# SSD products of four heads in one visit, retention's products by kind, an extra step between retention's scores and their use, and later last blocks of the norms

## The chip, the cores and the metric

The kernel runs on one core of one Trainium2 chip. TensorE (PE) does the matrix products, VectorE (DVE), ScalarE (ACT) and GpSimd (POOL) the rest, and SyncE (SP) issues the transfers. The metric is the device time of one execution in microseconds (us), the median of several runs.

## The reference

A hybrid encoder of two layers is applied to a prompt of 512 tokens and a sample of 256 tokens, with a width of 1024, in fp32. The even layer mixes with an SSD scan of 16 heads (two groups of 8, both directions) and with retention of 8 heads (both directions), the odd layer with dilated attention and a gMLP. Each layer then has a squared-ReLU MLP. Every mixer and MLP stands between an RMS norm before and one after. Cut to what matters here:

```python
def ssd_chunked(x, log_a, bm, cm):                      # chunks of 128 tokens
    ...
    cb = jnp.einsum('bclgn,bcsgn->bcgls', cc, bc)
    y_diag = jnp.einsum('bcgels,bcsgep->bclgep', cb[:, :, :, None] * decay, xc)
    ...
    y_off = jnp.einsum('bclgn,bcgepn,bcgel->bclgep', cc, h_in, jnp.exp(a_cs).astype(x.dtype))
    return (y_diag + y_off).reshape(Bsz, L, G, E, P)

def retention_chunked(q, k, v, log_gamma):
    ...
    scores = jnp.einsum('bclhd,bcshd->bchls', qc, kc) * dmat
    y_in = jnp.einsum('bchls,bcshv->bclhv', scores, vc)
    ...
    y_cross = jnp.einsum('bclhd,bchdv,hl->bclhv', qc, r_in, q_decay)
    return (y_in + y_cross).reshape(Bsz, L, H, DV)

def even_mixer(h, in_proj, ...):
    ...
    y = y_f + y_b + xs * d_skip.reshape(SSD_GROUPS, SSD_HPG, 1).astype(xs.dtype)
    y_ssd = gated_group_rms(y.reshape(Bsz, S, SSD_WIDTH), z, ssd_norm_w)
    ...
    y_ret = head_group_norm(r, ret_gn_w) * jax.nn.silu(g)
    return jnp.concatenate([y_ssd, y_ret], axis=-1) @ out_proj

def trunk(x, norm_mix_pre, norm_mix_post, ...):
    for i in range(DEPTH):
        h = rms_norm(x, norm_mix_pre[i])
        ...
        x = x + rms_norm(mix, norm_mix_post[i])
        h = rms_norm(x, norm_ffn_pre[i])
        f = jnp.square(jax.nn.relu(h @ ffn_w1[i])) @ ffn_w2[i]
        x = x + rms_norm(f, norm_ffn_post[i])
    return x
```

## The kernel before

**Precision.** A big projection multiplies operands split in two parts (whi and wlo of a weight, h or mh in a high and a low part), so that one product is three matmuls (L156 to L158, L191 to L193, L212 to L214). L118 loads a weight, ACT makes its high part (L121) and DVE the low one (L122). SSD and retention products are plain fp32, each issued as a pair.

**What sets the order.** PE's order is written out by hand: it is the order of the code. `weave(steps, fill, per)` walks through the steps of a special stage (SSD or retention) and puts `per` steps of a projection's matmuls, the fill, behind each `yield`. A fill step is 6 matmuls. When the fill is used up, the steps stand alone. The other engines' orders come from a scheduler that follows the code and takes `high_priority()` work first. All transfers go through SP's one queue, in order. PSUM has three pools: dps with 3 tiles for projections, mps with 3, tps with 2. A tile is held until its last reader is done.

**SSD** (`ssd`, once per head group g). Chunks of 128 tokens, six in all. Before the products of chunk c, the code makes the products C B' (cb, L1297) and the masks of chunk c + 1: `ssd_decay` loads decays (rr), masks and exponentiates them, POOL adds the two directions (L1360), DVE multiplies by cb (L1361, the mask product) and adds the D-skip on the diagonal (four steps of L1365). The products L1315 then run in four visits per chunk, two heads each: terms ea with hf (state from the left), ea with hb (from the right), rr with xtok (inside the chunk), 64 output rows a head, so the tile is 128*64. The norm of a chunk has two halves (L1374 sums the squares; L1382 spreads the result); they stand between the products of the next chunk and ahead of those of the one after.

**Retention** (`ret`, once per head group of four). First the states (rl with rs, L1507, and on DVE L1516 and L1522), then for each of six chunks `ret_chunk`: transposes L1537 and L1543, scores L1552 (64 rows), the masked scores sct on DVE (L1557), half of the norm of the chunk before, products L1565 (sct with v) and L1566 (qst with the states ri; 64 rows in the first and the last chunk of a sequence, 128 otherwise, since ri stacks the two directions). `ret_norm` normalises ys (L1579 to L1588), transposes (L1591) and stores the mix tile. Fill of retention group 0 are the projections of group 1 (`E.gates(1)`, `E.ret_proj`), 3.6 steps each, and fill of group 1 is three quarters of the output projection (`out(0)` to `out(2)`, which load mix tiles, mh, L1612 to L1618), 2.4 each. The last quarter follows group 1, with tiles of its own.

**Norms behind a projection** (`PostNorm`). Of each of three token blocks the squares are summed (ACT L456, POOL L460, PE L276), then `end` makes r (L285 to L290), scales (L486), adds the residual (L490) and makes the next projection's h (L364, L365). For the last block, `pre.rest()` calls it from within the next projection, behind its first dense unit of 24 matmuls (`units_a` L145, `units_b` L179). In the last norm of the program nothing follows: eight scales L486 and eight adds L490 end the kernel.

```python
                if i == j == 0 and not pre.first:
                    pre.rest()
```

## Time and profile before

| what | value |
|---|---|
| three runs, median | 2264.56 us (2263.85 to 2268.53) |
| profiled execution, its own time | 2263.86 us |
| its span, first to last instruction | 2262.1 us |
| mean granted clock of PE | 0.990 |
| PE busy (matmuls) | 2191.4 us, 97% |
| PE weight loads | 2027.0 us, 90% |
| DVE busy | 1679.8 us, 74% |
| ACT busy | 1056.9 us, 47% |
| POOL busy | 614.4 us, 27% |

A matmul's duration in a row of the trace is longer than the distance to the next one, since matmuls overlap in the array; the stream is read from the starts. PE's stream has no slack of its own, so what counts are the places where the distance between two starts is larger than it should be.

### The profile page before, as it was taken

Reading aid. Unit: us, or ns where it says so; the run is one execution under the profiler, and the core shown is the slowest. Engines: PE = TensorE matmul, PEld = TensorE weight load, DVE = VectorE, ACT = ScalarE, POOL = GpSimd, SP = SyncE. Lnnn points to the kernel's source line nnn. Section 1 sums busy time; section 2 is a strip of 40 time slices with the busy share of each in tenths; the row PEclk is TensorE's granted clock in tenths of the full one; section 3 lists DMA queues with packets and bytes.
Section 4 is the critical chain, followed back from the end, with each engine's and each line's share of the span. In section 5 each row is a group of like instructions: output and inputs, shape, how many; then the busy total and the mean of one; then the engine's idle time right before and its main releaser. Section 6 shows DMA issues by size and latency. Waiting matters only on the chain.

```text
span 2262.1 us, 39158 instructions
## 1 busy us (share of the span) xinstructions
PE 2191.4 (97%) x14360; PEld 2027.0 (90%) x14360; DVE 1679.8 (74%) x3538; ACT 1056.9 (47%) x2132; POOL 614.4 (27%) x617
## 2 busy tenths in 40 slices
PE   8998999999999999999999999999999999999997
PEld 7877888998889999989988988888988999999987
DVE  8969858646658776687677858788767776687676
ACT  6646455334335544454244415555655544454242
POOL 2335234311104144311404030011004154311404
PEclk9999999999999999999999999999999999999999
DMA  4435235446434343454353345444634343454342
GB/s 150 120 125 170 88 102 167 149 136 192 136 107 142 97 142 123 143 184 145 114 170 119 109 140 171 147 157 133 193 112 132 104 137 123 143 189 140 114 152 89
DMA packets 188897, 311.23 MB, mean 138 GB/s; under 512 B 18913, under 2 KB 119329, under 8 KB 188705
## 3 DMA queue, kind: packets, MB, share of 16 engines
q1 hardware_dynamic: 188704, 308.73, 43.1%
q8 instruction: 113, 1.85, 0.3%
q14 instruction: 80, 0.65, 0.1%
HBM read 234.64 MB, written 74.02 MB: 136 GB/s over the span
## 4 chain that ended last, share of the span: by engine, by line
PE 62%; DVE 18%; DMA 9%; issue 4%; ACT 4%; POOL 2%; SPq 1%; POOLq 0%; ACTq 0%; DVEq 0%
PE dps L156 4%; PE dps L157 4%; PE dps L158 4%; PE dps L212 4%; PE dps L213 4%; PE dps L214 4%; PE dps L191 3%; PE dps L192 3%; PE dps L193 3%; PE dps L663 3%; PE dps L664 3%; PE dps L665 3%; DMA raw<-in_f 2%; DVE wlo L122 2%; PE mps L665 2%
## 5 line engine op out<-in xcount | busy, mean ns | idle before, releaser
L212 PE MATMUL dps<-mh,whi 128*128 128x256 f32 (+1 forms) x800 | 271.6, 340 | 1.4 <-DVE acc L223 1.1
L213 PE MATMUL dps<-mh,whi 128*128 128x256 f32 (+1 forms) x800 | 266.1, 333 | 0.0
L214 PE MATMUL dps<-mh,wlo 128*128 128x256 f32 (+1 forms) x800 | 265.3, 332 | 0.0
L191 PE MATMUL dps<-whi,h 128*128 128x256 f32 x864 | 260.8, 302 | 0.2 <-ACT rv L1466 0.2
L156 PE MATMUL dps<-h,whi 128*128 128x256 f32 (+1 forms) x728 | 251.8, 346 | 0.0
L192 PE MATMUL dps<-wlo,h 128*128 128x256 f32 x864 | 246.3, 285 | 0.0
L193 PE MATMUL dps<-whi,h 128*128 128x256 f32 x864 | 246.3, 285 | 0.0
L158 PE MATMUL dps<-h,wlo 128*128 128x256 f32 (+1 forms) x728 | 242.8, 333 | 0.0
L157 PE MATMUL dps<-h,whi 128*128 128x256 f32 (+1 forms) x728 | 242.1, 333 | 0.0
L122 DVE TENSOR_TENSOR wlo<-raw,whi 128x1024 fp32r<-128x1024 f32 x140 | 177.1, 1267 | 45.1 <-ACT whi L121 44.5
L121 ACT ACTIVATE whi<-raw 128x1024 fp32r<-128x1024 f32 x140 | 147.6, 1056 | 123.4 <-PE dps L157 49.6
L191 PEld LDWEIGHTS dps<-whi,h 128*128 128x128 f32 x864 | 166.6, 193 | 11.3 <-issue 8.5
L192 PEld LDWEIGHTS dps<-wlo,h 128*128 128x128 f32 x864 | 166.9, 193 | 3.3 <-issue 2.2
L212 PEld LDWEIGHTS dps<-mh,whi 128*128 128x128 f32 x800 | 152.7, 191 | 18.8 <-DVE acc L223 2.7
L193 PEld LDWEIGHTS dps<-whi,h 128*128 128x128 f32 x864 | 166.8, 193 | 0.0
L214 PEld LDWEIGHTS dps<-mh,wlo 128*128 128x128 f32 x800 | 152.4, 191 | 14.8
L213 PEld LDWEIGHTS dps<-mh,whi 128*128 128x128 f32 x800 | 152.9, 191 | 13.3
L460 POOL TENSOR_TENSOR sq<-sq 128x256 f32<-128x256 f32 x79 | 64.9, 822 | 342.9 <-ACT sq L456 342.3
L156 PEld LDWEIGHTS dps<-h,whi 128*128 128x128 f32 x728 | 138.1, 190 | 17.0 <-issue 4.9
L157 PEld LDWEIGHTS dps<-h,whi 128*128 128x128 f32 x728 | 138.3, 190 | 13.6 <-issue 1.7
L158 PEld LDWEIGHTS dps<-h,wlo 128*128 128x128 f32 x728 | 137.9, 189 | 13.6
L223 DVE TENSOR_TENSOR acc<-acc,dps 128x512 f32<-128x512 f32 (+1 forms) x208 | 100.5, 486 | 66.0 <-PE dps L214 65.7
(380 smaller groups left out, 6323.7 us busy)
## 6 DMA issues: line engine op xcount, KB each, us to landing
raw<-in_f SPq DMA_DIRECT2D x128, 512.0 KB, 3.8
hidD<-hc SPq DMA_DIRECT2D x104, 192.0 KB, 1.9
xt<-hidD SPq DMA_DIRECT2D x40, 384.0 KB, 3.6
rr<-acsD SPq DMA_DIRECT2D x48, 256.0 KB, 3.6
raw<-in_evB SPq DMA_DIRECT2D x24, 512.0 KB, 3.7
rl<-retD SPq DMA_DIRECT2D x48, 256.0 KB, 2.8
raw<-hidD SPq DMA_DIRECT2D x24, 512.0 KB, 3.9
stk<-qkD SPq DMA_DIRECT2D x96, 128.0 KB, 2.8
```

The costliest lines, as they stand in the source:

```text
L121: nc.scalar.activation(out=hi, in_=raw, func=AF.Copy)
L122: nc.vector.tensor_tensor(out=lo, in0=raw, in1=hi, op=ALU.subtract)
L156: nc.tensor.matmul(o, lhsT=hi[:, k, :], rhs=hh[k][:, sl], start=k == 0, stop=False)
L157: nc.tensor.matmul(o, lhsT=hi[:, k, :], rhs=hl[k][:, sl], start=False, stop=False)
L158: nc.tensor.matmul(o, lhsT=lo[:, k, :], rhs=hh[k][:, sl], start=False, stop=k == NKT - 1)
L191: nc.tensor.matmul(o, lhsT=hh[k][:, sl], rhs=hi[:, k % 4, :], start=k == 0, stop=False)
L192: nc.tensor.matmul(o, lhsT=hh[k][:, sl], rhs=lo[:, k % 4, :], start=False, stop=False)
L193: nc.tensor.matmul(o, lhsT=hl[k][:, sl], rhs=hi[:, k % 4, :], start=False, stop=k == NKT - 1)
L212: nc.tensor.matmul(o, lhsT=hi[:, k, ms], rhs=hh[k][:, sl], start=k == 0, stop=False)
L213: nc.tensor.matmul(o, lhsT=hi[:, k, ms], rhs=hl[k][:, sl], start=False, stop=False)
L214: nc.tensor.matmul(o, lhsT=lo[:, k, ms], rhs=hh[k][:, sl], start=False, stop=k == 3)
L665: nc.tensor.matmul(o, lhsT=lo[:, k, :], rhs=hh[k], start=False, stop=last and k == 3, **f)
```

## The change

It has five parts.

1. `units_a` and `units_b` call `pre.rest()` one dense unit later: behind the second one and not the first. It concerns the MLP of both layers and the odd layer's input projection.
2. In the last block of the last norm, r is written to a PSUM tile (tps) instead of SBUF.
3. SSD: the two `yield` of two heads move behind those of four heads, so a chunk has two visits instead of four. The second half of a norm (`yield from spread`) moves from before the products to behind them. cb moves from tps to mps. The D-skip becomes one wide add per four heads, of a table (`di`) that 8 steps per group make ahead. The mask product gets high priority.
4. More tiles for s0 (6 instead of 4), and the last quarter's mh tiles lie in tiles that are dead by then.
5. Retention: a step (`yield`) now stands between scores and their use. All four qst products run first, then all four sct products. The half norm of the chunk before moves from between scores and use to behind the products and a step. The masked scores get high priority. Each chunk so has one more step, and takes one more helping of fill.

```diff
@@ units_a, units_b
-                if i == j == 0 and not pre.first:
+                if i == 0 and j == 1 and not pre.first:
                     pre.rest()
...
-                    if c == 0 and w is ws[0]:
+                    if c == 1 and w is ws[0]:
                         pre.rest()
@@ PostNorm.end
-        r = T.rstd(st, n, eps=None if self.eps is None else self.eps[s][:, c0 // CH:(c0 + n) // CH])
+        y = T.tps()[:, 0:n] if self.prek is None and b == BLOCKS[-1] else None
+        r = T.rstd(st, n, y, eps=None if self.eps is None else self.eps[s][:, c0 // CH:(c0 + n) // CH])
@@ Even.diagonals, called ahead of back_states(0) and, for group 1, behind the weave of ssd(0)
+    def diagonals(self, g):
+
+        self.di = []
+        for q in range(2):
+            t = self.pool.tile([128, 512], F32, tag="di", name="di", bufs=2)
+            for i in range(4):
+                h = 64 + 8 * g + 4 * q + i
+                self.nc.vector.tensor_scalar(out=t[:, 128 * i:128 * i + 128], in0=self.T.ident,
+                                             scalar1=self.rows[:, h:h + 1], scalar2=None, op0=ALU.mult)
+            self.di.append(t)
@@ ssd
-                cb = T.tps()
+                cb = T.mps()
...
-            yield from spread
             if c < 0:
                 continue
...
-                    yield
+
+                yield
+                yield
                 if q == 0:
                     yield from islice(half, 1)
+            yield from spread
             spread = half
@@ ssd_decay
-        nc.vector.tensor_tensor(out=v3(m), in0=v3(m), in1=cb[:, 0:128].unsqueeze(1).to_broadcast([128, 4, 128]),
-                                op=ALU.mult)
-        for i in range(4):
-            sl = slice(128 * i, 128 * i + 128)
-            nc.vector.scalar_tensor_tensor(out=m[:, sl], in0=T.ident, scalar=self.rows[:, 64 + h0 + i:65 + h0 + i],
-                                           in1=m[:, sl], op0=ALU.mult, op1=ALU.add)
+        with T.tc.high_priority():
+            nc.vector.tensor_tensor(out=v3(m), in0=v3(m), in1=cb[:, 0:128].unsqueeze(1).to_broadcast([128, 4, 128]),
+                                    op=ALU.mult)
+            nc.vector.tensor_tensor(out=m, in0=m, in1=self.di[q], op=ALU.add)
@@ ret_chunk
-        yield from half
+        yield
         y = T.mps()
         rows = slice(64 if c == c0 else 0, 64 if c == c1 else 128)
-        for h in range(4):
-            hs = slice(128 * h, 128 * h + 128)
-            nc.tensor.matmul(y[:, hs], lhsT=st[:, hs], rhs=v[:, hs], start=True, stop=False)
-            nc.tensor.matmul(y[:, hs], lhsT=qst[rows, hs], rhs=ri[rows, hs], start=False, stop=True)
+
+        for a, b, r, f in ((qst, ri, rows, True), (st, v, slice(0, 128), False)):
+            for h in range(4):
+                hs = slice(128 * h, 128 * h + 128)
+                nc.tensor.matmul(y[:, hs], lhsT=a[r, hs], rhs=b[r, hs], start=f and h == 0, stop=not f and h == 3,
+                                 skip_group_check=True)
...
         yield
+        yield from half
```

How the instructions move is seen at three places. In the changed kernel the lines are a little further down: L1315 is L1326, L1297 is L1308, L1382 is L1394, L1507 is L1519, L1565 and L1566 are L1580, L1586 and L1588 are L1601 and L1603, L1591 is L1606, L1618 is L1633.

PE, the products of one chunk's first four heads in SSD group 0, before (ea, hf, hb, rr and xtok as above; each row of L1315 is a pair of products, and issues two matmuls for each):

```order
L158 MATMUL dps<-h,wlo 128x512
L1315 MATMUL mps<-ea,hf 64x128 x2
L1315 MATMUL mps<-ea,hb 64x128 x2
L1315 MATMUL mps<-rr,xtok 64x128 x2
L156 MATMUL dps<-h,whi 128x512
...
L158 MATMUL dps<-h,wlo 128x512
L1315 MATMUL mps<-ea,hf 64x128 x2
L1315 MATMUL mps<-ea,hb 64x128 x2
L1315 MATMUL mps<-rr,xtok 64x128 x2
L156 MATMUL dps<-h,whi 128x512
```

The same after. The two visits have become one, and the six fill matmuls between them stand behind it:

```order
L158 MATMUL dps<-h,wlo 128x512
L1326 MATMUL mps<-ea,hf 64x128 x2
L1326 MATMUL mps<-ea,hb 64x128 x2
L1326 MATMUL mps<-rr,xtok 64x128 x2
L1326 MATMUL mps<-ea,hf 64x128 x2
L1326 MATMUL mps<-ea,hb 64x128 x2
L1326 MATMUL mps<-rr,xtok 64x128 x2
L156 MATMUL dps<-h,whi 128x512
```

PE, from the last products of retention group 0 (chunk 5) to the states of group 1, before. The row of L1591 is the norm's transposes of chunk 5 (sct is the tile that the normalised values are written to), rs the scaled keys; between the products and L1591 there are 72 fill matmuls of the projections, and the fill of group 1 (L212 on) begins with the states:

```order
L1565 MATMUL mps<-rl,sct 128x128
L1566 MATMUL mps<-ri,qst 128x128
L191 MATMUL dps<-whi,h 128x256
...
L1591 MATMUL tps<-ident,sct 128x128 x4
L191 MATMUL dps<-whi,h 128x256
...
L1507 MATMUL mps<-rl,rs 128x128 x4
L212 MATMUL dps<-mh,whi 128x512
...
L1507 MATMUL mps<-rl,rs 128x128 x4
```

The same after. Behind the products there is one step of fill (6 matmuls) and then the transposes of chunk 4; the states of group 1 follow, and only behind these, with 48 fill matmuls of L212 to L214 between and behind them, the transposes of chunk 5:

```order
L193 MATMUL dps<-whi,h 128x256
L1580 MATMUL mps<-ri,qst 128x128 x4
L1580 MATMUL mps<-rl,sct 128x128 x4
L191 MATMUL dps<-whi,h 128x256
...
L193 MATMUL dps<-whi,h 128x256
L1606 MATMUL tps<-ident,sct 128x128 x4
L1519 MATMUL mps<-rl,rs 128x128 x4
...
L1519 MATMUL mps<-rl,rs 128x128 x4
L212 MATMUL dps<-mh,whi 128x256
...
L1606 MATMUL tps<-ident,sct 128x128 x4
L212 MATMUL dps<-mh,whi 128x512
```

DVE, the last steps of the norm of chunk 5 (L1586, L1588) and what follows them, up to the first masked scores of group 1 (L1557), before. gx belongs to the gates, mh and wlo to the output projection, de to the decay tables of group 1:

```order
L1586 TENSOR_SCALAR sct<-ys,mv,rsq_y 128x128 x3
L1473 TENSOR_SCALAR gx<-dps,rc_101 128x256
L1586 TENSOR_SCALAR sct<-ys,mv,rsq_y 128x128
L1588 TENSOR_TENSOR sct<-sct,rl 128x512
...
L1618 TENSOR_TENSOR mh<-raw,mh 128x512
...
L1618 TENSOR_TENSOR mh<-raw,mh 128x256 x3
L122 TENSOR_TENSOR wlo<-raw,whi 128x1024
L1432 SCALAR_TENSOR_TENSOR de<-de,trif 128x128
...
L1618 TENSOR_TENSOR mh<-raw,mh 128x512 x3
...
L1557 TENSOR_TENSOR sct<-dm,mps 128x2x128 x2
```

The same place after: the norm's statistics, weights, decay tables and states of group 1 (ri) all stand ahead of the norm's last steps (L1601, L1603), for which the transposes of chunk 5 wait:

```order
L1633 TENSOR_TENSOR mh<-raw,mh 128x512
...
L1594 BN_STATS bs<-ys 128x6
...
L122 TENSOR_TENSOR wlo<-raw,whi 128x1024
...
L1444 SCALAR_TENSOR_TENSOR de<-de,trif 128x128
...
L1528 SCALAR_TENSOR_TENSOR ri<-ri,gam,mps 64x128 x5
L122 TENSOR_TENSOR wlo<-raw,whi 128x1024
L1528 SCALAR_TENSOR_TENSOR ri<-ri,gam,mps 64x128 x3
L265 SCALAR_TENSOR_TENSOR rsq_y<-rsq_u,rsq_y 128x4
L1601 TENSOR_SCALAR sct<-ys,mv,rsq_y 128x128 x4
L1534 SCALAR_TENSOR_TENSOR ri<-ri,gam 64x128
L1603 TENSOR_TENSOR sct<-sct,rl 128x512
```

## Rows read from the trace of the kernel before

**Rows 1.** The table of PE's waits: pool, line, what ended them; total, times, longest.

```profile
PE tps L276 <- POOL sq L460: 8.7, 4, 2.9
...
PE mps L1565 <- DVE sct L1557: 4.7, 2, 4.2
PE tps L1382 <- DVE rr L1361: 4.0, 2, 3.5
PE tps L1374 <- DVE rr L1361: 3.9, 3, 2.0
PE tps L1382 <- DVE diag L295: 3.8, 2, 2.6
PE tps L1591 <- DVE sct L1588: 3.6, 2, 3.2
```

**Rows 2.** PE's timeline at one SSD visit: start, duration, instruction.

```profile
145.44 0.39 PE L158 MATMUL dps<-h,wlo 128*128 128x512 f32 x1
...
146.02 0.39 PE L1315 MATMUL mps<-ea,hb 128*64 128x128 f32 x4
146.24 0.39 PE L1315 MATMUL mps<-rr,xtok 128*64 128x128 f32 x4
...
146.90 0.39 PE L157 MATMUL dps<-h,whi 128*128 128x512 f32 x1
147.12 0.40 PE L158 MATMUL dps<-h,wlo 128*128 128x512 f32 x1
```

**Rows 3.** Stretches: busy PE, PEld, DVE, ACT, POOL, then granted clock, DMA share, GB/s.

```profile
347.04:350.45 3.41, 3.41 (x23) 3.19 (x23) 3.41 (x11) 1.26 (x4) 0.00 (x0) 0.50 0.17 59
520.82:528.00 7.18, 7.18 (x63) 7.18 (x62) 6.76 (x29) 0.83 (x2) 1.18 (x2) 1.00 0.45 120
540.06:558.64 18.58, 14.82 (x96) 12.79 (x94) 17.86 (x41) 14.16 (x31) 6.80 (x6) 1.00 0.75 236
558.66:568.90 10.24, 9.79 (x33) 7.91 (x34) 2.85 (x16) 1.84 (x4) 0.00 (x0) 0.50 0.36 126
1234.50:1241.33 6.83, 5.85 (x23) 5.50 (x24) 6.83 (x14) 3.79 (x10) 3.56 (x4) 0.50 0.63 195
```

**Rows 4.** PE's timeline at the products of two retention chunks and at scores.

```profile
446.00 0.71 PE L1552 MATMUL mps<-qkt 64*128 64x128 f32 x8
...
450.48 0.39 PE L1565 MATMUL mps<-rl,sct 128*128 128x128 f32 x2
...
452.39 0.28 PE L192 MATMUL dps<-wlo,h 128*128 128x256 f32 x1
...
478.36 0.39 PE L1565 MATMUL mps<-rl,sct 128*128 128x128 f32 x2
...
481.82 0.28 PE L192 MATMUL dps<-wlo,h 128*128 128x256 f32 x1
```

**Rows 5.** DVE's timeline: a mask product, a weight split, and the tail.

```profile
345.75 0.69 DVE L1361 TENSOR_TENSOR rr<-rr,tps 128x512 f32<-128x512 f32 x1 [2.84 <-POOL rr L1360]
...
673.72 1.23 DVE L122 TENSOR_TENSOR wlo<-raw,whi 128x1024 fp32r<-128x1024 f32 x1 [0.55 <-ACT whi L121]
...
2251.42 0.42 DVE L289 SCALAR_TENSOR_TENSOR rstd<-tps,rstd 128x256 f32<-128x256 f32 x1 [1.94 <-ACT rstd L287]
...
2252.42 3.47 DVE L486 SCALAR_TENSOR_TENSOR acc<-acc,pv,rstd 128x256 f32<-128x256 f32 x5
```

**Rows 6.** PE's timeline at four places that wait or are waited for.

```profile
340.61 0.38 PE L1297 MATMUL tps<-bc 128*128 128x128 f32 x2
...
559.12 0.80 PE L1565 MATMUL mps<-rl,sct 128*128 128x128 f32 x2 [4.23 <-DVE sct L1557]
...
662.98 0.60 PE L1591 MATMUL tps<-ident,sct 128*128 128x128 f32 x4
...
1235.48 1.22 PE L276 MATMUL tps<-sq,ones 128*128 128x256 f32 x2 [2.87 <-POOL sq L460]
```

**Rows 7.** The h of the odd layer's last block: min, median, max ns, first and last start.

```profile
L365 DVE SCALAR_TENSOR_TENSOR h<-acc,pv,h x16: 460/476/957, 1237.8 to 1254.6; 128x256 fp32r<-128x256 f32 x16
```

More of the change, by code (lines that the diff above doesn't have):

```diff
@@ L1085, in s0 @@
     def s0(self, name):
-        return self.pool.tile([128, 512], F32, tag="s0", name=name, bufs=4)
+        return self.pool.tile([128, 512], F32, tag="s0", name=name, bufs=6)
     def proj_dt(self, b, w):
@@ L1556, in ret_chunk @@
             ev = "p (a b l) -> p a b l"
-            nc.vector.tensor_tensor(
-                out=st.rearrange(ev, a=2, b=2)[:, :, i], in0=self.dm.rearrange(ev, a=2, b=2)[:, :, i],
-                in1=sc[i][:, 0:256].rearrange("p (a l) -> p a l", a=2), op=ALU.mult)
-        yield from half
+            with T.tc.high_priority():
+                nc.vector.tensor_tensor(
+                    out=st.rearrange(ev, a=2, b=2)[:, :, i], in0=self.dm.rearrange(ev, a=2, b=2)[:, :, i],
+                    in1=sc[i][:, 0:256].rearrange("p (a l) -> p a l", a=2), op=ALU.mult)
+        yield
         y = T.mps()
         rows = slice(64 if c == c0 else 0, 64 if c == c1 else 128)
-        for h in range(4):
-            hs = slice(128 * h, 128 * h + 128)
-            nc.tensor.matmul(y[:, hs], lhsT=st[:, hs], rhs=v[:, hs], start=True, stop=False)
-            nc.tensor.matmul(y[:, hs], lhsT=qst[rows, hs], rhs=ri[rows, hs], start=False, stop=True)
+        for a, b, r, f in ((qst, ri, rows, True), (st, v, slice(0, 128), False)):
[3 more added lines that the diff above has]
+                                 skip_group_check=True)
         ys = pool.tile([128, 512], F32, tag="xtok", name="ys", bufs=7)
@@ L1675, in even_layer @@
         for _ in range(13): next(fill)
+        E.diagonals(0)
         weave(E.back_states(0), fill, 4)
@@ L1679, in even_layer @@
         weave(E.ssd(0), fill, SR0)
+        E.diagonals(1)
         run(E.ssd_proj(1))
@@ L1699, in tiles, with dead @@
             return pool.tile([128, n], F32R, tag=tag, name="fw", bufs=bufs)[:, 0:512]
-        t = by_seq([[pool.tile([128, NT], F32R, tag="mh", name="mh", bufs=4) for _ in range(4)], []])
-        t0 = [pool.tile([128, 512], F32R, tag="s0", name="mh", bufs=4) for _ in range(4)]
-        t1 = [x[:, 256 * j:256 * j + 256] for x in [pool.tile([128, 512], F32R, tag="hf", name="mh", bufs=2) for _ in range(2)]
-              for j in range(2)]
-        place = [[t[0][0], t0], [t[1][0], t1]]
+        def dead(tag, n, bufs, count):
+            return [pool.tile([128, n], F32R, tag=tag, name="mh", bufs=bufs) for _ in range(count)]
+        t0 = dead("s0", 512, 6, 6) + dead("hf", 512, 2, 2)
+        t1 = [x[:, 256 * j:256 * j + 256] for x in dead("di", 512, 2, 2) + dead("bc0", 512, 3, 1) for j in range(2)]
+        t1 += dead("bc1", 256, 3, 2)
+        place = [[t0[0:4], t0[4:8]], [t1[0:4], t1[4:8]]]
         run(T.quarter(I["evO"][3], mix_load(T, E.mixD, 3, place=place), acc, False, pn))
```

## The prediction

> **What bounds the kernel now.** I read the page first: PE is busy 2191.4 of 2262.1 us, the next engine, DVE, 1679.8 (the table above). So the time is PE's stream of matmuls plus the places where that stream stumbles, and an edit elsewhere counts only through them. In the steady stream a matmul of 512 columns starts every 0.22 to 0.23 us, one of 256 every 0.12. The stumbles are of three kinds.
> - Waits. The table of PE's waits names what ended each [rows 1]: at L276 the squares of a norm (POOL), at L1565 and L1591 retention's scores and norm (DVE sct), at L1374 and L1382 the SSD norm (DVE).
> - Changes of tile shape, which no table of waits has. The reader is to look at the starts, not the durations: from 145.44 to 146.90 PE issues two matmuls of 512 columns and three groups of four small ones [rows 2]. The middle group takes 0.22 (146.02 to 146.24), a 512-column matmul the same (146.90 to 147.12), so a steady stream would take some 1.12. The visit took 1.46: **0.34 more**.
> - Half clock behind a wait. [...] The shortest such stretch is 3.41 [rows 3] and costs 1.7.
>
> **A. SSD products of four heads in one go.** The order has 48 visits before and 24 after, each twice as long. 24 x 0.34 = **8.2 us** less. Low end 0, if the price is one per matmul and not per visit.
>
> **B. Retention's products by kind.** A chunk whose qst tiles have 128 rows takes 1.91 (450.48 to 452.39), one with 64 rows 3.46 (478.36 to 481.82), for the same sixteen matmuls and one fill matmul [rows 4]. The difference, 1.55, is four round trips between the shapes at 0.39; by kind one round trip stays. Eight of the twelve chunks have 64 rows (the first and the last of both sequences, two head groups): 8 x 3 x 0.39 = **9.3 us**. Low end 0, if 64-row matmuls are slow by themselves. [...]
>
> **C. The SSD norm's second half behind the products, and cb in mps.** The mask product L1361 reads cb, so cb's tps tile is held until then: at 345.75, where DVE had waited 2.84 for POOL's add [rows 5]. L1382 and L1374, which want a tps tile, waited for it in both head groups. Of their waits in [rows 1], 2.6, 2.0, 1.1 and 0.5 lie in group 0, with two stretches of 3.41 at half clock, together 9.6; 3.5 and 0.8 in group 1, with one stretch, together 6.0; 1.2 is in the deferred norm of group 0 and stays. After, cb takes one of the three mps tiles, and its matmul for chunk 3 (L1308 after) waits for the mask product of chunk 2: a **new wait**. In the trace of before that matmul stood at 340.61 [rows 6], and the mask product it would wait for ended at 346.44, 5.8 later. High priority moves the product forward on DVE, but the POOL add ahead of it needs a DMA. I take 4 and 1.7 of clock in group 1 and 2 in group 0: 15.6 - 7.7 = **7.9 us**. Bounds 15.6 (no new wait) and 0 (5.8 with its clock in both). The 96 small D-skip steps taken from DVE, the 24 wide adds and the 16 table steps lie beside DVE's idle time and count for nothing; if they didn't, it would be in the gain's favour.
>
> **D. Retention, group 0.** The smaller waits of L1565 and L1591 in [rows 1], 0.5 and 0.4, go, since the extra step puts fill between: **0.9 us**.
>
> **E. Retention, group 1, and the last quarter of the output projection.** What goes: the wait of 4.2 at 559.12, where sct came late because DVE had mh splits ahead of it, half of the 9.79 busy behind it (4.9), and the wait of 3.2 at L1591 with a stretch of clock (1.7): 14.0 [rows 1, 3, 6]. What comes, by the order shown above, since the extra step per chunk uses the fill up earlier:
> - *The norm of chunk 5 of group 0.* Its transposes, L1606, now stand behind four state matmul groups of group 1 and 54 fill matmuls, some 12.4 us after its products. In between DVE does the norm (6.76 busy in 520.82 to 528.00) and what it did from 540.06 to 558.64 (17.86 busy: weight and mh splits, decay tables, states) [rows 3], 24.6 less some 3 that still stand behind, so 21.6 against 12.4. The first splits can run earlier; I take a wait of 8 and 1.7 of clock. Bounds 0 (all that work runs early) and 13.
> - *The start of quarter 3.* The last transposes stood at 662.98 [rows 6]. What quarter 3 needs comes from them in a row: the store of the last mix tile, its load behind that on SP, the weights behind that, then the split, whose low half was there at 674.95 (673.72 and 1.23 [rows 5]), 12.0 us later. 114 fill matmuls, some 20 us, hid it. SP's order is the same after, and only 30 fill matmuls are left, 12 of 512 and 18 of 256 columns, 5.2 us with the transposes 5.7. PE waits **6.3 us**, and 1.7 of clock. Bounds 3 and 10.
>
> 14.0 - 9.7 - 8.0 = **-3.7 us**: this part gets slower.
>
> **F. Later last blocks.** The three waits at L276 ahead of a projection are 8.7 less the 1.2 of the tail, 7.5 [rows 1]; behind them the clock was half for 6.83 in the odd layer [rows 3] and for one stretch in layer 0, 5.1 lost. In all 12.6. One dense unit (24 matmuls, 2.85) now goes ahead of each, as long as the longest wait of 2.9. What is late next is the block's h: in the odd layer L276 ran at 1235.48 [rows 6] and the last h ended at about 1255.1 [rows 7], 19.6 later; block 2 starts after 144 matmuls now, 17.3, and reads the last h some 2.5 behind the first. The margin is 0.2. I take **11.0 us**; bounds 7.5 and 12.6. With the cover gone, each us of lateness is lost, and half a stretch of clock.
>
> **G. The tail.** Five scales L486 take 3.47, 0.69 each, while POOL adds; L289, which reads tps, takes 0.42 [rows 5]. With r in PSUM, eight scales at 0.45 end some **1.8 us** earlier; low end 0. [...]
>
> **Sum:** 8.2 + 9.3 + 7.9 + 0.9 - 3.7 + 11.0 + 1.8 = **35.4 us**. The profiled execution took 2263.86, which leaves 2228.5; the median of the three runs is 0.7 above it: **2229.2**.
>
> **Rivals.**
> 1. *The new waits don't come.* DVE and POOL run ahead while PE does the longer visits, and cb, the norm of chunk 5 and quarter 3 are in time. For it: DVE idles a quarter of the span. The sum gains 7.7 + 9.7 + 8.0 = 25.4: 2204, and with half of that 2217. Against it: the store, load and split behind the last transposes have no idle time in them.
> 2. *The new waits are half as large again or twice,* with the clock low behind them as at 558.66: 12.7 to 25.4 more, 2242 to 2255. Against it: fill still stands in each of these places.
> 3. *The change of shape is paid by the matmul:* A and B give nothing, 17.5, and the time is 2247. Against it: the middle group of [rows 2] and the scores of [rows 4] are fast.
> 4. *Slower than before: half clock in all of retention group 1.* Each chunk's L1606 now follows the next chunk's products after one step of fill. If DVE is late at every chunk, PE idles in each, and the clock, low for 10.24 us after one wait [rows 3], stays low over the six chunks. At half clock each us of steady work costs a half: the gain of 35 is used up at 70 us of it. With 82 us: 2270. Against it: DVE's work per chunk is no larger than before, and one stretch over 10 us is all that the trace has.
>
> **From the cases to the numbers.** The forecast with its bounds, 2221 to 2240: 0.50. Rival 1, 2204 to 2221: 0.18. Rival 2, 2240 to 2258: 0.20. Rival 3: 0.05. Rival 4: 0.04. Within 0.2% of before, 4.5 us, about what a measurement of this kernel can tell from no change: 0.03, with the end of rival 2 0.04. The range 2210 to 2250 leaves out a third of rival 1 and of rival 2, 0.13, and the 0.07 of the last two.
>
> **What would show it.** Right: 24 visits with L1326 and 0.34 at each; 64-row chunks of L1580 in 2.3 instead of 3.46; no wait for the mask product at L1394 but one at L1308; no wait for sct near 559, but one at the L1606 behind retention group 0 and one of about 6 at the first L212 of quarter 3; at L276 only the tail's wait. Wrong: none of these three new waits (rival 1), several long stretches at half clock between 535 and 670 (rivals 2 and 4), chunks of L1580 still at 3.4 (rival 3), or block 2 of the odd layer waiting for h.

## The result and the profile after

The changed kernel takes **2235.86 us** (median of 4 runs, 2234.51 to 2237.87) against 2265.44 us before; the ratio is 0.9867, 95% interval 0.9852 to 0.9883. That is 29.6 us less, where 35.4 were forecast, and lies within the range. The profiled execution is the slowest of the four, 2237.87, so rows account for 26 us.

The page of the changed kernel, its first lines:

```profile
span 2236.0 us, 39067 instructions
...
PE 2172.7 (97%) x14360; PEld 2020.8 (90%) x14360; DVE 1667.0 (75%) x3482; ACT 1054.9 (47%) x2132; POOL 612.9 (27%) x617
```

PE's waits after, the table that answers to [rows 1] (in the same columns; cb's matmul, L1308 in the prediction, is L1309):

```profile
PE dps L212 <- ACT whi L121: 5.3, 1, 5.3
PE tps L1386 <- POOL gsq L1340: 4.9, 2, 4.4
PE tps L1606 <- DVE sct L1603: 4.8, 1, 4.8
PE mps L1309 <- DVE zl L1337: 2.3, 1, 2.3
...
PE dps L156 <- ACT fr L985: 1.6, 2, 0.8
...
PE dps L191 <- ACT gv L1780: 1.3, 1, 1.3
...
PE tps L1394 <- DVE diag L295: 1.2, 1, 1.2
PE tps L276 <- POOL sq L460: 1.2, 1, 1.2
...
PE mps L1326 <- DVE zl L1337: 1.1, 1, 1.1
...
PE dps L214 <- DVE wlo L122: 0.5, 1, 0.5
```

Nearly every wait of [rows 1] is gone: sct at L1565 and in group 1 at L1591, the mask product at L1374 and L1382, the squares at L276 but for the tail's 1.2. In their place stand new ones, first among them the start of quarter 3 (L212), the SSD norm's sum of squares (L1386) and the norm of retention's chunk 5 (L1606).

The stream itself, PE's timeline at a visit and at a chunk with 64 rows, which answer to [rows 2] and [rows 4]:

```profile
144.58 0.39 PE L158 MATMUL dps<-h,wlo 128*128 128x512 f32 x1
144.90 0.44 PE L1326 MATMUL mps<-ea,hf 128*64 128x128 f32 x4
...
146.70 0.40 PE L157 MATMUL dps<-h,whi 128*128 128x512 f32 x1
...
471.11 0.28 PE L193 MATMUL dps<-whi,h 128*128 128x256 f32 x1
471.32 1.16 PE L1580 MATMUL mps<-ri,qst 64*128 64x128 f32 x8
472.41 1.16 PE L1580 MATMUL mps<-rl,sct 128*128 128x128 f32 x8
...
473.52 0.28 PE L192 MATMUL dps<-wlo,h 128*128 128x256 f32 x1
```

The visit now does twice the work in 2.12 us (144.58 to 146.70); steady would be 2 x 0.23 + 6 x 0.22 = 1.78, so the price of a visit is still 0.34, paid half as often. Read in the same way from the starts, every visit of both kernels that neither waits nor runs at half clock, with 8, 12, 16 or 24 matmuls, has a price of 0.33 to 0.35. The chunk takes 2.20 (471.32 to 473.52) instead of 3.46. Counted from the fill matmul ahead of it (471.11), which takes in the whole change of shape, it is 2.41, against 3.58 for the old order and 2.03 for a chunk of 128 rows, both in the kernel before: one round trip of 0.38 is left of four.

Where the time went shows in the lengths of the stages, each from the start of one matmul to that of another that both kernels have, read from the timelines of PE: SSD group 0 (first cb to first cb of group 1), SSD group 1 (to the first state of retention), retention with the output projection (to its first L276 in the last quarter), the MLP of layer 0 and the start of the odd layer (to the first L276 on psq), and the rest up to the last norm's first L276. Norms that the change moves lie in the last two. The matmul between these two columns stands one dense unit, 2.9 us, later in every kernel here but the one before and e3, so for these two columns only the sum is to be compared. e1 to e12 are the experiments below:

```
            SSD 0   SSD 1   retention   to first psq      rest
before      184.3   104.1     288.7          567.9        957.4
after       179.8    98.0     279.9          566.3        953.6
e1          181.2   100.9     280.0          563.7        954.3
e2          179.5    97.1     288.3          564.2        952.7
e3          179.0    96.5     279.8          567.9        958.2
e4          180.0    96.5     265.6          564.1        955.7
e5          179.4    97.4     280.8          564.4        956.2
e6          178.3    96.3     280.3          566.0        955.8
e7          179.8    96.4     273.5          564.9        955.5
e8          179.8    98.9     279.6          562.9        956.2
e9          182.3    97.7     280.1          566.5        955.5
e10         192.6   100.5     279.7          564.3        955.7
e11         189.6    98.7     269.0          564.6        954.6
e12         183.0   101.9     279.1          565.4        954.6
```

The SSD part gained 10.6, retention 8.8, the norms 5.4 in the last two columns, the tail 1.4 (below): 26.2 together. Stages whose code is the same differ by about 1.5 from one kernel's profile to the next, in SSD group 0 by up to 3.3 (e9 against e3) and in the last two columns by up to 3.6; the profiles of the changed kernel and of e9 have a stretch at half clock in the MLP (3.41 us) that the others don't have.

The norms can be read more sharply, from one fill matmul shortly ahead of each of the three moved norms to one well behind it, the same two in each kernel (in the changed one they start at 697.54 and 733.92, 1191.19 and 1280.48, 1712.23 and 1749.11):

```
            MLP of layer 0   input of the odd layer   its MLP
before           39.54               92.40             38.41
after            36.38               89.29             36.88
e3               39.56               92.41             38.44
```

In the other eleven kernels these are 36.36 to 36.45, 89.29 to 89.69 and 36.63 to 36.92. So the later norms bring 3.16 + 3.11 + 1.53 = 7.8, of which 5.4 is left in the last two columns.

### The profile page after: what moved, and what is told of

The parts are those of the page before. It is cut to its first block, busy times and chain, and to the rows that moved or that the text cites. A ratio compares the mean times of both kernels' runs of the same rounds, so it can differ in the third digit from the quotient of the medians.

```text
span 2236.0 us, 39067 instructions
## 1 busy us (share of the span) xinstructions
PE 2172.7 (97%) x14360; PEld 2020.8 (90%) x14360; DVE 1667.0 (75%) x3482; ACT 1054.9 (47%) x2132; POOL 612.9 (27%) x617
## 4 chain that ended last, share of the span: by engine, by line
PE 67%; DVE 18%; DMA 6%; ACT 4%; issue 4%; POOL 1%; SPq 0%; DVEq 0%; POOLq 0%; ACTq 0%
PE dps L212 5%; PE dps L213 5%; PE dps L214 5%; PE dps L156 4%; PE dps L157 4%; PE dps L158 4%; PE dps L191 4%; PE dps L192 3%; PE dps L193 3%; PE dps L664 3%; PE dps L665 3%; PE dps L666 3%; DVE acc L487 3%; PE mps L664 2%; PE mps L665 2%
## 5 line engine op out<-in xcount | busy, mean ns | idle before, releaser
L212 PE MATMUL dps<-mh,whi 128*128 128x256 f32 (+1 forms) x800 | 272.4, 340 | 8.2 <-ACT whi L121 5.3
L214 PE MATMUL dps<-mh,wlo 128*128 128x256 f32 (+1 forms) x800 | 265.5, 332 | 0.5 <-DVE wlo L122 0.5
L191 PE MATMUL dps<-whi,h 128*128 128x256 f32 x864 | 258.3, 299 | 1.5 <-ACT gv L1780 1.3
L156 PE MATMUL dps<-h,whi 128*128 128x256 f32 (+1 forms) x728 | 251.5, 346 | 0.0
L212 PEld LDWEIGHTS dps<-mh,whi 128*128 128x128 f32 x800 | 152.9, 191 | 26.2 <-ACT whi L121 5.5
L191 PEld LDWEIGHTS dps<-whi,h 128*128 128x128 f32 x864 | 166.4, 193 | 9.4 <-issue 4.9
L214 PEld LDWEIGHTS dps<-mh,wlo 128*128 128x128 f32 x800 | 152.3, 190 | 15.5 <-DVE wlo L122 0.8
L156 PEld LDWEIGHTS dps<-h,whi 128*128 128x128 f32 x728 | 137.9, 189 | 16.6 <-issue 4.4
```

Of the source, the lines that this page charges most:

```text
L156: nc.tensor.matmul(o, lhsT=hi[:, k, :], rhs=hh[k][:, sl], start=k == 0, stop=False)
L191: nc.tensor.matmul(o, lhsT=hh[k][:, sl], rhs=hi[:, k % 4, :], start=k == 0, stop=False)
L212: nc.tensor.matmul(o, lhsT=hi[:, k, ms], rhs=hh[k][:, sl], start=k == 0, stop=False)
L214: nc.tensor.matmul(o, lhsT=lo[:, k, ms], rhs=hh[k][:, sl], start=False, stop=k == 3)
```

## The experiments

All are edits of the changed kernel, timed like it against the kernel before; a difference of two of their ratios is uncertain by some 0.2%, 5 us, so that the stages' lengths and the waits decide what the times leave open. No run takes back part 4 alone, or one of the high priorities of the change, so what these bring is not shown.

**e1, SSD products in four visits again.**

```diff
                                              start=n == 0, stop=n == len(terms) - 1)
-
-                yield
-                yield
+                    yield
```

> The changed kernel with the SSD products in four visits per chunk again (the two steps stand between the pairs of heads as before); all else as changed. Theory (a price of 0.34 us per visit): 24 visits more, so 8.2 us more than the changed kernel's 2235.9, about 2244, with no other wait moved. Rival 1 (the price is per matmul): 2236. Rival 2 (the longer visits are what makes the SSD norm's sums wait for POOL, 4.9 us and some 5 us of half clock behind them): these go, and the time is 2234 to 2236 although the visits cost 8 more.

Measured: 2244.40 us, ratio 0.9902 (0.9887 to 0.9918), 7.9 above the changed kernel. Its two SSD stages are 4.3 longer than in the changed kernel's profile; against the six profiles with the changed SSD code (the changed kernel's, e2, e3, e4, e7, e9) they are 2.1 to 6.6 longer, 5.0 in the mean. The wait at the sum of squares is 1.5 instead of 4.9:

```profile
PE mps L1326 <- DVE zl L1335: 2.0, 1, 2.0
...
PE tps L1384 <- POOL gsq L1338: 1.5, 1, 1.5
...
PE mps L1326 <- DVE rr L1374: 1.3, 1, 1.3
```

Others are longer, 3.3 at L1326 where the changed kernel has 1.1. So the price per visit holds (0.34 in the starts of e1's visits too), though not "with no other wait moved", and rival 2 has a part in it: the longer visits do bring the sum of squares closer to its use, and some 3 us of the 8.2 go back into waits.

**e2, retention's products head by head again.**

```diff
-        for a, b, r, f in ((qst, ri, rows, True), (st, v, slice(0, 128), False)):
-            for h in range(4):
...
+        for h in range(4):
+            hs = slice(128 * h, 128 * h + 128)
+            nc.tensor.matmul(y[:, hs], lhsT=st[:, hs], rhs=v[:, hs], start=True, stop=False)
+            nc.tensor.matmul(y[:, hs], lhsT=qst[rows, hs], rhs=ri[rows, hs], start=False, stop=True)
```

> The changed kernel with retention's products in the old order (one sct product, one qst product, head by head), the steps and fill as changed. Theory (a round trip between 128-row and 64-row matmuls costs 0.39 us, three more in each of eight chunks): 9.3 us more, about 2245, and a 64-row chunk takes 3.46 us instead of 2.2. Rival (64-row matmuls are slow by themselves, or the old stalls of these chunks came from waits): 2236, chunk still at about 2.2.

Measured: 2241.17 us, ratio 0.9891 (0.9876 to 0.9906), 5.4 above; the retention stage is 8.4 longer, and no other stage. A chunk's sixteen matmuls and the fill matmul behind them take the old time again, 3.45 (470.97 to 474.42), with 0.41 to 0.42 from one pair to the next (PE's timeline of e2):

```profile
470.97 0.39 PE L1579 MATMUL mps<-rl,sct 128*128 128x128 f32 x2
471.28 0.49 PE L1580 MATMUL mps<-ri,qst 64*128 64x128 f32 x2
471.70 0.49 PE L1579 MATMUL mps<-rl,sct 128*128 128x128 f32 x2
...
474.20 0.38 PE L191 MATMUL dps<-whi,h 128*128 128x256 f32 x1
474.42 0.28 PE L192 MATMUL dps<-wlo,h 128*128 128x256 f32 x1
```

The eight 64-row matmuls by kind start within 1.09 (471.32 to 472.41 in the fence above). It is the change between shapes that costs, not the 64 rows: theory, a little under its 9.3.

**e3, the last blocks' norms one dense unit earlier again.**

```diff
-                if i == 0 and j == 1 and not pre.first:
+                if i == j == 0 and not pre.first:
...
-                    if c == 1 and w is ws[0]:
+                    if c == 0 and w is ws[0]:
```

> The changed kernel with the last blocks' norms behind the first dense unit again (three places). Theory (three waits of 7.5 us in all and 5 us of half clock come back, 1.6 us of new waits for the projection's own evacuations go): 8 to 11 us more, 2244 to 2247. Rival (the waits were hidden work that is now only elsewhere): within 3 us of 2236.

Measured: 2245.59 us, ratio 0.9910 (0.9894 to 0.9925), 9.7 above. The three lengths around the norms are those of the kernel before (table above), 7.9 longer than in the changed kernel. The waits at L276 are back (8.8 in all), and those at L156 and L191 for the projection's own evacuations are gone. Theory, at its low end by the lengths, within it by the time.

**e4, less fill per retention step.**

```diff
-RR0 = 3.6
-RR1 = 2.4
+RR0 = 2.98
+RR1 = 1.99
```

> The changed kernel with fewer fill steps per retention step, 2.98 instead of 3.6 and 1.99 instead of 2.4, so that 35 steps use up as much fill as 29 did. Theory (the waits at the transposes behind retention group 0, 4.8 us, and at the start of the last quarter, 5.8 us, with 6.8 us lost to half clock, come from fill used up early): they go, 2219 to 2224. Rival (less fill per step uncovers the masked scores and the norm in every chunk): new waits of some 0.5 us in each of twelve chunks, 2225 to 2236. Third (the waits come from DVE's order, whatever the fill): 2236.

Measured: **2223.35 us**, ratio 0.9815 (0.9799 to 0.9832), 42 us below the kernel before and 12 below the changed one: the fastest version here. Its retention stage is 14.3 shorter. The waits at L1606 and at the first weights of quarter 3 are gone, and no stretch at half clock is left in the stage (the mean granted clock of the span is 0.998, 0.992 in the changed kernel); the only wait of over 0.5 us there is this one (PE's timeline):

```profile
536.22 1.04 PE L1580 MATMUL mps<-rl,sct 128*128 128x128 f32 x6 [0.71 <-DVE sct L1570]
```

Theory, within its range. Lower rates alone take both waits away, so they came from fill used up early.

**e5, high priority for the multiply by z.**

```diff
-            nc.vector.tensor_tensor(out=z, in0=z, in1=ym, op=ALU.mult)
+            with T.tc.high_priority():
+                nc.vector.tensor_tensor(out=z, in0=z, in1=ym, op=ALU.mult)
```

> The changed kernel with high priority for the multiply of the SSD products by z (L1337), which stands up to 10 places earlier on DVE. Theory (this multiply comes late on DVE, so the products' tile of mps is held and POOL's sum of squares is late; the waits at L1309, 2.3, and L1326, 1.1, are for the tile, that at L1386, 4.9, for the sum): the first two go and part of the third, with half clock 3 to 7 us less, 2229 to 2233. Rival (cb's tile waits for the mask product, as the prediction had it): L1309 still waits some 2 us, 2236.

Measured: 2237.75 us, ratio 0.9869 (0.9852 to 0.9885), no change. The wait at L1309 went, the one at L1386 fell to 3.2, and a new one came two microseconds behind the old place, at chunk 2's products in group 1, for their own mask product:

```profile
339.26 0.44 PE L1326 MATMUL mps<-ea,hf 128*64 128x128 f32 x4 [1.84 <-DVE rr L1377]
```

The theory named the right tile (what held cb back was the products' tile, not the mask product's), but the mask's chain is as late as that, so that the wait only moved.

**e6, both D-skip tables ahead of everything** (four tiles instead of two).

```diff
+        E.di = {}
         E.diagonals(0)
+        E.diagonals(1)
...
-        E.diagonals(1)
         run(E.ssd_proj(1))
```

> The changed kernel with the D-skip tables of both head groups made ahead of everything (four tiles instead of two). Theory (the eight table steps of group 1, at 205 to 210 us ahead of the last multiply by z on DVE, make the 4.4 us wait at L1386): this wait falls below 1 us and 3.4 us of half clock behind it go, the 2.3 at L1309 stays: 5 to 8 us less, 2228 to 2231. Rival (POOL's own queue makes the sum late): the wait stays at over 3 us, 2236.

Measured: 2236.89 us, ratio 0.9866 (0.9852 to 0.9881), no change that the times can tell; SSD group 0 is 1.5 shorter, no more than profiles of the same code differ. Its longest wait at L1386 is 2.5 instead of 4.4:

```profile
PE tps L1386 <- POOL gsq L1340: 3.8, 2, 2.5
```

So the table steps make 1.9 of the 4.4 (it was 4.4 to 4.5 in e2, e3, e4 and e7 too, and 3.1 in e9, where PE had waited 2.9 for ACT shortly before). The rest is DVE's: in e6 the multiply by z stands behind the chain of the norm before and rotary steps, 3.8 us behind the start of the last products, and POOL idled ahead of the sum (DVE's and POOL's timelines of e6):

```profile
211.01 0.68 DVE L1337 TENSOR_TENSOR zl<-zl,mps 128x512 f32<-128x512 f32 x1
212.43 0.72 POOL L1340 TENSOR_TENSOR gsq<-gsq 128x256 f32<-128x256 f32 x1 [0.53 <-ACT gsq L1339]
```

The theory had the cause of not quite half of the wait; POOL's queue, the rival's cause, is not what is left.

**e7, retention without the extra step,** products by kind kept.

```diff
-        yield
+        yield from half
         y = T.mps()
...
         yield
-        yield from half
```

> The changed kernel with retention's steps as before (no step between scores and use, the half norm there again, 29 steps per group), products by kind kept. Theory of the prediction (the step trades 14.0 us of waits and half clock for 17.7 us of others): the waits at the transposes behind group 0 and at the start of the last quarter go, waits of 4 at L1580 and 3 at L1606 in group 1 come back, and the time is 2 to 6 us less, 2230 to 2234. Rival (the step is a gain by itself): over 2238.

Measured: 2230.63 us, ratio 0.9840 (0.9826 to 0.9855), 5 to 6 below the changed kernel; the retention stage is 6.4 shorter. The old waits are back, the first smaller than in [rows 1] (4.2), the second as large (3.2) (PE's timeline):

```profile
538.45 0.79 PE L1580 MATMUL mps<-rl,sct 128*128 128x128 f32 x2 [2.90 <-DVE sct L1570]
...
581.37 0.78 PE L1605 MATMUL tps<-ident,sct 128*128 128x128 f32 x4 [3.31 <-DVE sct L1602]
```

The step at the old rates is a loss, as forecast; with the rates of e4 it is a gain, 7.9 in the stage (265.6 against 273.5). e7's stage is also 15.2 shorter than that of the kernel before, more than B's 8.4: among other things the first masked scores of group 1 wait 2.9 instead of 4.2, with the clock at half for 6.83 and not 10.24. Whether their high priority does this isn't shown.

**e8, cb in tps again.**

```diff
-                cb = T.mps()
+                cb = T.tps()
```

> The changed kernel with cb in tps again, the norm's second half still behind the products. Theory of the prediction (cb's tile, held until the mask product, is what the norm's matmuls waited for): waits of 2 to 4 us at L1386 and L1394 come back, L1309 waits no more for mps: 2238 to 2246. Rival (the later place of the second half alone takes the waits away): L1394 doesn't wait, L1309's 2.3 goes, 2232 to 2236.

Measured: 2238.50 us, ratio 0.9873 (0.9858 to 0.9888), no change that can be told. The 2.3 at L1309 is gone, and chunk 2's sum waits for a mask product, as sums did in the kernel before:

```profile
359.62 0.58 PE L1386 MATMUL tps<-ones,gsq 128*128 128x1 f32 x4 [2.98 <-DVE rr L1376]
```

Moving cb to mps trades one wait for another, then, and L1394 doesn't wait for the mask either way. Of the theory the wait at L1386 came, of the rival L1394 without one.

**e12, the second half of the SSD norm ahead of the products again,** cb in mps.

```diff
+            yield from spread
             if c < 0:
                 continue
...
-            yield from spread
             spread = half
```

> The changed kernel with the second half of the SSD norm ahead of the products again, cb in mps and all else as changed. Theory (the later second half is what took away the waits at L1394 for the diagonal and the mask product, and the cause of the new waits is the late multiply by z behind it): waits of 2 to 3 us at L1394 come back, those at L1386 (4.9) and L1309 (2.3) shrink by half or more: within 4 us of 2236. Rival 1 (cb in mps alone frees L1394, and the later half only makes the new waits): 4 to 9 us less. Rival 2 (the later half is worth all of what is gained in the SSD part): L1394 waits 6 us or more again, 2240 to 2246.

Measured: 2249.03 us, ratio 0.9922 (0.9902 to 0.9943), 12.5 above; the SSD stages are 7.1 longer. One wait is larger than any that the SSD part had before:

```profile
185.54 0.79 PE L1394 MATMUL tps<-diag,ones 128*128 128x128 f32 x2 [8.65 <-DVE diag L295]
```

L1386 no longer waits, and L1309 still waits 1.9. With two visits per chunk the norm's chain on DVE comes too late for the early place, so the later one is needed: rival 2, 3 us beyond its times.

**e10, the first half of the SSD norm one visit later too,** and **e11**, e4 with the tables of e6 and this edit.

```diff
-                if q == 0:
+                if q == 1:
                     yield from islice(half, 1)
```

> The changed kernel with the first half of the SSD norm (the sum of squares on TensorE, L1386) behind the second visit of the next chunk, with 24 matmuls more of fill ahead of it. Theory (DVE's and POOL's work for the sum simply needs more time, since the products come in fewer, longer visits): the 4.9 us of waits at L1386 fall to about 1 and the half clock behind them goes, 4 to 8 us less, 2228 to 2232. Rival (the wait moves, to the norm's second half L1394 or to the tile for the next products, as it did when the multiply by z was moved): within 2 us of 2236.

> The changed kernel with the lower fill rates (2.98 and 1.99), the D-skip tables made ahead and the first half of the SSD norm one visit later. If the gains add up (14 us in retention, 1.5 from the tables, 4 to 8 in the SSD part): 2213 to 2219. If the SSD wait only moves: 2220 to 2223.

Measured: e10 2252.75 us, ratio 0.9938 (0.9914 to 0.9962), 16 above; e11 2234.22 us, ratio 0.9860 (0.9835 to 0.9884). The wait for the sum went and came back larger, as 5.3 for the diagonal and 10.0 for ACT (table of e10's waits):

```profile
PE dps L191 <- ACT rx L1461: 10.0, 5, 3.1
...
PE tps L1394 <- DVE diag L295: 6.8, 3, 5.3
```

The wait moves, as the rival had it, but neither theory nor rival had it grow, and e11 came 11 above the larger of its two forecasts. SSD group 0 grew to 192.6. In e11 retention still gained (269.0), and the SSD part lost that again (189.6). ACT evacuates the fill (L1461) late because its order has the masks' exponentials (L1371) first, and these wait for POOL's masking (ACT's timeline of e10, at the wait of 3.1):

```profile
190.83 0.70 ACT L1371 ACTIVATE rr<-rr,bias 128x128 f32<-128x128 f32 x2 [1.12 <-POOL rr L1367]
191.43 0.46 ACT L1461 ACTIVATE rx<-dps,rc 128x256 f32<-128x256 f32 x1
```

What makes POOL late there stays open.

**e9, r of the last norm in SBUF.**

```diff
-        y = T.tps()[:, 0:n] if self.prek is None and b == BLOCKS[-1] else None
+        y = None
```

> The changed kernel with r of the last norm in SBUF again. Theory (scales that read r from SBUF beside POOL's adds take 0.69 us, from PSUM about 0.5): the stretch from the last matmul to the end is 12.4 us as before the change, against 11.0 after it, and the scales take 0.69 to 0.75 us each. Rival (the tail was shortened by something else, such as the clock or the transfers): it stays at 11.0.

One run, 2243.80 us. Up to the last norm it is 4.6 longer than the changed kernel's profile, so only the tail is compared. From the first scale to the end of the span it takes 9.6 (2232.30 to 2241.9), the kernel before 9.7 (2252.42 in [rows 5] to 2262.1), the changed one 8.3 (2227.70 to 2236.0). DVE's scales in the changed kernel, and in e9, which takes the same 3.47 for five as [rows 5]:

```profile
2227.23 0.43 DVE L290 SCALAR_TENSOR_TENSOR tps<-rstd 128x256 f32<-128x256 f32 x1
2227.70 2.05 DVE L487 SCALAR_TENSOR_TENSOR acc<-acc,pv,tps 128x256 f32<-128x256 f32 x5
```

```profile
2231.83 0.43 DVE L290 SCALAR_TENSOR_TENSOR rstd<-rstd 128x256 f32<-128x256 f32 x1
2232.30 3.47 DVE L487 SCALAR_TENSOR_TENSOR acc<-acc,pv,rstd 128x256 f32<-128x256 f32 x5
```

All eight scales of the tail, shortest, median and longest in ns, first in the kernel before, then in the changed one, then in e9:

```profile
L486 DVE SCALAR_TENSOR_TENSOR acc<-acc,pv,rstd x8: 471/940/946, 2252.4 to 2257.7; 128x256 f32<-128x256 f32 x8
L487 DVE SCALAR_TENSOR_TENSOR acc<-acc,pv,tps x8: 468/476/481, 2227.7 to 2231.7; 128x256 f32<-128x256 f32 x8
L487 DVE SCALAR_TENSOR_TENSOR acc<-acc,pv,rstd x8: 473/939/948, 2232.3 to 2237.6; 128x256 f32<-128x256 f32 x8
```

Theory, and the rows say more than it: the 0.69 is a mean of two kinds. With r in SBUF, the five scales that start while a POOL add is running take 0.94, the other three 0.47 to 0.49. With r in PSUM all eight take 0.47 to 0.48, beside POOL's adds or not.

## Why the prediction was right, and which terms were off

The forecast case came: all three new waits of the prediction are in the trace, though one for another tile, and the gain of 29.6 is 35.4 less 5.8. Most of what is missing is in C and F. Step by step:

- **A, visits, 8.2.** Right in mechanism and price (0.34 in the rows of both kernels). Some of it, about 3 us, is given back by the waits that longer visits bring (e1); they are counted under C here.
- **B, products by kind, 9.3.** Right: 8.4 in e2's stage, 2.20 per chunk where 2.3 was expected (a part of the remaining round trip lies ahead of the first product).
- **C, 7.9.** This is the step that was mis-sized. A and C together were to bring 16.1, and the SSD stages show 10.6 (8.4 to 12.9 over the six profiles with this code), so C brought 2.4 (0 to 5). The waits add up to the same: the 15.6 went as forecast, since of the SSD waits of [rows 1] only the deferred 1.2 is left, but what came is 4.9 at L1386, 2.3 at L1309, 1.1 at L1326 and 6.83 and 3.41 at half clock (0.50 granted, PE busy throughout), half of that lost: 13.4, where 7.7 was taken. The step "cb ... waits for the mask product of chunk 2" named the wrong tile: L1309 waited 2.3 for the tile of the products, held by the multiply by z. And the larger new wait, 4.4 at L1386, isn't in the prediction at all. Its cause stands on four engines' timelines (changed kernel, PE, DVE, ACT, POOL):

```profile
206.59 0.39 PE L1326 MATMUL mps<-rr,xtok 128*64 128x128 f32 x4
...
214.43 0.75 PE L1386 MATMUL tps<-ones,gsq 128*128 128x1 f32 x3 [4.38 <-POOL gsq L1340]
...
206.68 1.25 DVE L1286 TENSOR_SCALAR di<-ident,rows 128x128 f32<-128x128 f32 x1
...
211.56 0.67 DVE L1337 TENSOR_TENSOR zl<-zl,mps 128x512 f32<-128x512 f32 x1
...
212.27 0.63 ACT L1339 ACTIVATE gsq<-zl 128x512 f32<-128x512 f32 x1 [1.83 <-DVE zl L1337]
...
212.21 1.27 POOL L1374 TENSOR_TENSOR rr<-rr 128x512 f32<-128x512 f32 x1
213.44 0.94 POOL L1340 TENSOR_TENSOR gsq<-gsq 128x256 f32<-128x256 f32 x1
```

  The products started their last group at 206.59, the multiply by z came 5 us later, behind table steps (L1286), rotary steps and the chain of the norm before. ACT's squares were there at 212.90, and POOL's sum of them stood another 0.5 behind the add of a mask (L1374). "The 96 small D-skip steps ... count for nothing" was wrong where the eight table steps of group 1 stand in the middle of group 0: 1.9 of the 4.4 (e6). What C brings comes from the later half (e12), not from cb's pool (e8).
- **D and E, 0.9 and -3.7.** Right, and the numbers near: the wait at L1606 was 4.8 (8 was taken, within its bounds), at quarter 3 5.3 and 0.5 for the low half (6.3 was taken). For the first, DVE had the norm done 17.9 after the products' end, not 21.6 (PE's and DVE's timelines):

```profile
513.72 1.16 PE L1580 MATMUL mps<-rl,sct 128*128 128x128 f32 x8
...
532.05 0.68 DVE L1603 TENSOR_TENSOR sct<-sct,rl 128x512 f32<-128x512 f32 x1
```

  Each wait brought a stretch at half clock:

```profile
531.96:538.79 6.83, 6.00 (x18) 4.96 (x19) 4.64 (x12) 2.58 (x7) 0.00 (x0) 0.50 0.79 233
658.25:665.08 6.83, 4.01 (x17) 3.72 (x18) 4.55 (x8) 4.63 (x8) 0.00 (x0) 0.50 0.86 287
```

  The stage gained 8.8 with B's 8.4 in it, so the rest is about zero where -2.8 was forecast. Some of the difference is luck: the kernel before waited once for rs at the states, a wait that the prediction left out and that of all later profiles only e11's has:

```profile
PE mps L1507 <- POOL rs L1484: 1.7, 1, 1.7
```

  That the two waits come from fill used up early is shown by e4, and that the step at the old rates costs more than it gives by e7.
- **F, 11.0.** Right in mechanism, too large: 7.8 by the three lengths around the norms, 7.9 against e3, 9.7 by e3's time. The three waits went. But PE, being earlier, then waits for the evacuations of its own projection, 2.9 in all: 0.8 twice at L156, 1.3 at L191, in the table above. Neither the kernel before nor e3 has these waits, and the prediction had no term for them. And the half clock was counted in full where PE stood still in part of the stretch (5.85 busy of 6.83 in [rows 3]), which is 0.5. Block 2 of the odd layer didn't wait for h, so the cover held.
- **G, 1.8.** The last scale ends 4.4 behind the start of the first, 6.3 before: 1.8 as worked out. 1.4 arrived at the end of the span, behind the last adds and stores. The reading behind it was half right: the slow scales were those that start beside a POOL add (e9), not all. A scale with r in PSUM takes 0.47 to 0.48 (0.45 was taken), as one all in SBUF does where no add runs beside it (0.47 to 0.49).

Of the rivals, the first (no new waits) fell with the three waits, and e4 shows what it would have been worth in retention; the second (larger new waits) is true of the SSD part, 13.4 for 7.7, and not of retention; the third fell with e1 and e2; the fourth with the stretches at half clock, none over 6.83 ahead of the tail.

## What to carry to other kernels

A step that is added to a woven stage takes a helping of fill with it: lower the rate by as much, or the end of the stage stands bare (12 us here, e4 against the changed kernel). Matmuls of another tile shape were paid for by the visit here (0.34 us each), so put them together, but look at what reads their results: fewer and longer visits bring the reader closer (the sum of squares waited 4.9 in the changed kernel, 1.5 in e1). A wait that is removed by moving one instruction often stands at the next link of the same chain (e5, e8, e10); follow the chain to its slowest engine before moving anything.

## What the runs showed of the hardware

- A matmul stream that goes from 128*128 tiles to 128*64 and back pays 0.34 us, whether 8, 12, 16 or 24 matmuls stand between; from 128*128 to 64*128 and back 0.38 to 0.39, of which a chunk by kind pays one.
- A VectorE scale of 128x256 with all its operands in SBUF takes 0.94 us when it starts while GpSimd adds in SBUF, and 0.47 to 0.49 otherwise; with r in PSUM it takes 0.47 to 0.48 in both cases (tails of the kernel before, the changed one and e9).
- In the changed kernel's profile PE's granted clock fell from 1.00 to 0.50 for 6.83 us at each of the three waits of 4.4 to 5.3 us, and for 3.41 at the wait of 2.3 (L1309). It is not the same each time: at the wait of 4.4 to 4.5 (L1386) it was 3.41 in e3 and e4, and at L1309 e2, e3 and e4, with the same code and a wait of 2.4 to 2.6, have none.
